# A row softmax on one core: whole-tile maxima, a broadcast multiplication in six tiles, and a new order for the last tiles

## Chip, cores and metric

One core of a Trainium2 chip. In the profiles DVE is VectorE, ACT is ScalarE and SP is SyncE; a q behind an engine (ACTq) marks its queue, from which its DMAs are issued. The metric is device time in microseconds (us) of one execution; 35 executions of the kernel before lay between 317.39 and 318.83 us, all but one within 0.3% of 317.7. "Span" is the profiled part of an execution, some 2 us shorter than the time.

## The reference

```python
x: (32, 512, 1024) float32;  temperature = 0.5

scaled  = x / temperature
shifted = scaled - max(scaled, axis=-1, keepdims=True)
exp_x   = exp(shifted)
return exp_x / sum(exp_x, axis=-1, keepdims=True)
```

16384 rows of 1024 numbers: 67.1 MB are read and 67.1 MB written.

## The kernel before

The rows are cut into 16 tiles of 128 partitions x 8 rows x 1024 (4 MB each), kept in six buffers. A tile is worked on in two groups of four rows. For each group DVE takes the maxima of the rows and makes a bias of them, ACT computes the exponentials row by row (in place, with the row's sum as a by-product), and DVE inverts the sums and multiplies each row. A tile goes out by one DMA, issued in ACT's queue; right after it in the program stands the load that reuses a buffer, in SP's queue.

```python
TILES = [[8]] * 16
BUFS = 6
GROUP = 4
...
    def maximum(g):
        ...
        nc.vector.tensor_reduce(out=top, in_=tiles[i][:, a : a + k, :], axis=..., op=extreme)
        nc.vector.tensor_scalar_mul(bias, in0=top, scalar1=-scale)

    def exponential(g):
        for b in range(k):
            nc.scalar.activation(tiles[i][:, a + b, :], tiles[i][:, a + b, :], Exp,
                                 bias=bias[:, b : b + 1], scale=scale, accum_out=sums[:, b : b + 1])

    def divide(g):
        nc.vector.reciprocal(recip, sums)
        for b in range(k):
            nc.vector.tensor_scalar_mul(tiles[i][:, a + b, :], in0=tiles[i][:, a + b, :],
                                        scalar1=recip[:, b : b + 1])

    def store(g):                      # after the last group of a tile
        nc.scalar.dma_start(out=dram(of, i)..., in_=tiles[i]...)
        load()                         # the next load, into a buffer that comes free
...
    nc.vector.addr_align(128, offset=0, max_nops=0)
    nc.scalar.addr_align(128, offset=0, max_nops=0)
    for _ in range(BUFS):
        load()
    for g in range(len(groups) + 1):
        if g < len(groups):
            maximum(g)
            exponential(g)
        if g > 0:
            divide(g - 1)
            store(g - 1)
```

So in program order the multiplication and the store of a group come behind the maximum and the exponentials of the next group.

## Time and profile before

| before | |
|---|---|
| time, median of 3 | 317.68 us (317.51 to 318.83) |
| span | 315.6 us |
| DVE busy | 235.5 us (75%) |
| ACT busy | 149.6 us (47%) |
| share of the span that the two DMA queues' packets took | 98.9% |

Most of the lines on which this reading rests are in the prediction below. To them belong the costliest groups and the DMA issues of the page. A group line has the source line, engine, operation, what is written and read, shape and count, then busy us and mean ns of one, then the idle time in front of it with what ended it. A DMA line has the size of one and the median time from issue to landing.

```profile
L70 DVE TENSOR_REDUCE top<-xt 128x4 f32<-128x4096 f32 x32 | 141.3, 4416 | 62.2 <-DMA xt<-in_x_dram 62.2
L93 DVE TENSOR_SCALAR xt<-xt,recip 128x1024 f32<-128x1024 f32 x128 | 87.7, 749 | 1.1
...
xt<-in_x_dram SPq DMA_DIRECT2D x16, 4096.0 KB, 50.2
out_dram<-xt ACTq DMA_DIRECT2D x16, 4096.0 KB, 38.4
```

The maxima are DVE's largest item, and in front of them DVE stands idle for 62.2 us in all, waiting for loads. A load takes 50 us to land although 4 MB at the 433 GB/s that before moved from 90 to 280 us are 9.7 us: it queues.

### The profile page before, as it was taken

What the parts mean: (1) busy time and instruction counts of PE and PEld (TensorE: products, weight loads), DVE (VectorE), ACT (ScalarE), POOL (GpSimd) and SP (SyncE); (2) the same over time, 40 slices, a digit from 0 to 9 for tenths busy, and PEclk for the clock granted to TensorE, in tenths of its full rate; (3) what the DMA queues carried; (4) which work ended last, traced back from release to release, by engine and by line L of the source; (5) the groups of instructions that cost most, each with busy time, mean ns of one, the idle gap of its engine ahead of it and who ended that gap; (6) DMA issues with size and microseconds to landing.
All of it is one profiled execution on the core that took longest, in us unless ns stands there. A gap on an engine that the chain in (4) does not pass through costs nothing.

```text
span 315.6 us, 622 instructions
## 1 busy us (share of the span) xinstructions
DVE 235.5 (75%) x224; ACT 149.6 (47%) x257; POOL 0.2 (0%) x4
## 2 busy tenths in 40 slices
DVE  0299999999789494994939949498594976949720
ACT  0176666666626255361553615546065560645500
POOL 0000000000000000000000000000000000000000
DMA  8999999999999999999999999999999999999996
GB/s 330 415 448 415 386 457 407 461 411 453 424 440 432 432 432 429 444 424 453 415 454 407 457 407 457 403 461 403 461 403 461 403 462 403 461 419 444 428 436 278
DMA packets 4613, 134.26 MB, mean 425 GB/s; under 512 B 512, under 2 KB 512, under 8 KB 512
## 3 DMA queue, kind: packets, MB, share of 16 engines
q1 hardware_dynamic: 2304, 67.11, 49.7%
q10 hardware_dynamic: 2304, 67.11, 49.2%
q14 instruction: 5, 0.04, 0.0%
HBM read 67.11 MB, written 67.11 MB: 425 GB/s over the span
## 4 chain that ended last, share of the span: by engine, by line
DVE 72%; another core or an unknown queue 15%; DMA 4%; ACT 3%; issue 1%; DVEq 0%
DVE top L70 43%; DVE xt L93 27%; DMA xt<-in_x_dram 4%; ACT xt L79 3%; DVE recip L91 1%; DVE bias L73 1%; DVEq L150 0%
## 5 line engine op out<-in xcount | busy, mean ns | idle before, releaser
L79 ACT ACTIVATE xt<-xt,bias 128x1024 f32<-128x1024 f32 x128 | 145.4, 1137 | 136.0 <-DVE recip L91 118.6
L70 DVE TENSOR_REDUCE top<-xt 128x4 f32<-128x4096 f32 x32 | 141.3, 4416 | 62.2 <-DMA xt<-in_x_dram 62.2
L93 DVE TENSOR_SCALAR xt<-xt,recip 128x1024 f32<-128x1024 f32 x128 | 87.7, 749 | 1.1
L79 ACT ACTIVATION_READ_ACCUMULATOR xt<-xt,bias 128x1 f32 x128 | 23.8, 186 | 0.0
L79 ACT ACT_TABLE_LOAD x1 | 1.3, 1283 | 13.5 <-DMA xt<-in_x_dram 13.5
L91 DVE RECIPROCAL recip<-sums 128x4 f32<-128x4 f32 x32 | 5.5, 171 | 2.1 <-ACT xt L79 2.1
L73 DVE TENSOR_SCALAR bias<-top 128x4 f32<-128x4 f32 x32 | 5.5, 170 | 1.1
L136 POOL MEMSET const-bfloat16-1.0<- 128x1 bf16 x1 | 0.1, 102 | 0.0
L136 POOL MEMSET const-uint8-127<- 128x1 uint8 x1 | 0.1, 102 | 0.0
L136 POOL MEMSET const-float32-0.0<- 128x1 f32 x1 | 0.1, 99 | 0.2 <-issue 0.2
L136 POOL MEMSET const-float32-1.0<- 128x1 f32 x1 | 0.1, 99 | 0.0
## 6 DMA issues: line engine op xcount, KB each, us to landing
xt<-in_x_dram SPq DMA_DIRECT2D x16, 4096.0 KB, 50.2
out_dram<-xt ACTq DMA_DIRECT2D x16, 4096.0 KB, 38.4
```

Source lines behind the costliest of these rows:

```text
L70: nc.vector.tensor_reduce(out=top, in_=tiles[i][:, a : a + k, :], axis=mybir.AxisListType.X, op=extreme)
L73: nc.vector.tensor_scalar_mul(bias, in0=top, scalar1=-scale)
L79: nc.scalar.activation(tiles[i][:, a + b, :], tiles[i][:, a + b, :], mybir.ActivationFunctionType.Exp, bias=bias[:, b : b + 1], scale=scal ...
L91: nc.vector.reciprocal(recip, sums)
L93: nc.vector.tensor_scalar_mul(tiles[i][:, a + b, :], in0=tiles[i][:, a + b, :], scalar1=recip[:, b : b + 1])
L136: nc = _bacc.Bacc("TRN2", target_bir_lowering=False, num_devices=1)
```

## The change

Its intent: fewer and longer instructions on DVE in the middle of the kernel, and at the end an order in which tile 13 and tile 14 are finished as soon as they can be. In tiles 2 to 13 the maximum is taken over all eight rows in one pass; in tiles 2, 4, .. 12 all eight rows are multiplied by one tensor_tensor with a broadcast factor; before tile 14 and before tile 15 the tile in front is divided and stored first; the two alignments (the addr_align lines) go.

```diff
-TILES = [[8]] * 16
+ROWS = 8
 BUFS = 6
-GROUP = 4
+PASSES = [[4, 4]] * 2 + [[8]] * 12 + [[4, 4]] * 2
+WHOLE = (2, 4, 6, 8, 10, 12)
+ALONE = 14
... (groups made from PASSES; a store still covers a whole tile)
     def divide(g):
         nc.vector.reciprocal(recip, sums)
+        if i in WHOLE:
+            xt = tiles[i][:, a : a + k, :]
+            nc.vector.tensor_mul(xt, xt, recip.unsqueeze(2).to_broadcast([P, k, d]))
+            return
         for b in range(k):
...
-        nc.vector.addr_align(128, offset=0, max_nops=0)
-        nc.scalar.addr_align(128, offset=0, max_nops=0)
         for _ in range(BUFS):
             load()
         for g in range(len(groups) + 1):
+            alone = g < len(groups) and groups[g][0] >= ALONE and groups[g][1] == 0
+            if g > 0 and alone:
+                divide(g - 1)
+                store(g - 1)
             if g < len(groups):
                 maximum(g)
                 exponential(g)
-            if g > 0:
+            if g > 0 and not alone:
                 divide(g - 1)
                 store(g - 1)
```

More of the change, by code (lines that the diff above doesn't have):

```diff
@@ L32 @@
     n, d = xf.shape
-    assert sum(sum(ks) for ks in TILES) * P == n
+    assert len(PASSES) * ROWS * P == n
     data = ctx.enter_context(tc.tile_pool(name="data", bufs=BUFS))
     stats = ctx.enter_context(tc.tile_pool(name="stats", bufs=4))
-    groups, first, r = [], [], 0
-    for i, ks in enumerate(TILES):
-        first.append(r)
-        r += sum(ks)
-        a = 0
-        for k in ks:
-            for b in range(0, k, GROUP):
-                m = min(GROUP, k - b)
-                groups.append((i, a + b, m, (a, k) if b + m == k else None))
-            a += k
+    groups = []
+    for i, ks in enumerate(PASSES):
+        assert sum(ks) == ROWS
+        for j, k in enumerate(ks):
+            groups.append((i, sum(ks[:j]), k))
     def dram(t, i):
-        k = sum(TILES[i])
-        block = t[P * first[i] : P * (first[i] + k), :]
-        return block.rearrange("(p k) d -> p k d", p=P, k=k)
+        block = t[P * ROWS * i : P * ROWS * (i + 1), :]
+        return block.rearrange("(p k) d -> p k d", p=P, k=ROWS)
     tiles, small = [], []
@@ L58, in load @@
         i = len(tiles)
-        if i < len(TILES):
-            xt = data.tile([P, sum(TILES[i]), d], f32, name="xt")
+        if i < len(PASSES):
+            xt = data.tile([P, ROWS, d], f32, name="xt")
             nc.sync.dma_start(out=xt, in_=dram(xf, i))
@@ L64, in maximum @@
     def maximum(g):
-        i, a, k, _ = groups[g]
+        i, a, k = groups[g]
         top, bias, sums, recip = (
@@ L75, in exponential @@
     def exponential(g):
-        i, a, k, _ = groups[g]
+        i, a, k = groups[g]
         bias, sums, _ = small[g]
@@ L88, in divide @@
     def divide(g):
-        i, a, k, _ = groups[g]
+        i, a, k = groups[g]
         _, sums, recip = small[g]
         nc.vector.reciprocal(recip, sums)
+        if i in WHOLE:
+            xt = tiles[i][:, a : a + k, :]
+            nc.vector.tensor_mul(xt, xt, recip.unsqueeze(2).to_broadcast([P, k, d]))
+            return
         for b in range(k):
@@ L97, in store @@
     def store(g):
-        i, _, _, part = groups[g]
-        if part:
-            a, k = part
-            nc.scalar.dma_start(out=dram(of, i)[:, a : a + k, :], in_=tiles[i][:, a : a + k, :])
-            if a + k == sum(TILES[i]):
-                load()
+        i, a, k = groups[g]
+        if a + k == ROWS:
+            nc.scalar.dma_start(out=dram(of, i), in_=tiles[i])
+            load()
     with tc.manual_schedule():
-        nc.vector.addr_align(128, offset=0, max_nops=0)
-        nc.scalar.addr_align(128, offset=0, max_nops=0)
         for _ in range(BUFS):
```

## The prediction

> **What bounds the kernel now.** I read the page first: the busy line, the slices, the queues.
>
> ```profile
> DVE 235.5 (75%) x224; ACT 149.6 (47%) x257; POOL 0.2 (0%) x4
> DVE  0299999999789494994939949498594976949720
> DMA  8999999999999999999999999999999999999996
> q1 hardware_dynamic: 2304, 67.11, 49.7%
> q10 hardware_dynamic: 2304, 67.11, 49.2%
> HBM read 67.11 MB, written 67.11 MB: 425 GB/s over the span
> ```
>
> No compute engine is near full, but the two DMA queues (loads on q1, stores on q10) took 49.7 + 49.2 = 98.9% of what 16 engines have in the span. Only 1.1% of 315.6 us, 3.5 us, is left, and both ends of the DMA row (8 and 6) use most of that up: nothing can move before the first issue, and the last bytes need a receipt.
>
> Then the chain of waits, which at first sight says the opposite.
>
> ```profile
> DVE 72%; another core or an unknown queue 15%; DMA 4%; ACT 3%; issue 1%; DVEq 0%
> 243.55 4.43 DVE top L70
> 251.03 4.34 DVE top L70
> 258.42 4.46 another core or an unknown queue
> 262.87 0.02 issue
> 262.90 4.43 DVE top L70
> ```
>
> 72% on DVE is where the trail was followed, not a bound: before each tile DVE stands still for 4.46 us. The waits name what it waits for:
>
> ```profile
> DVE top L70 <- DMA xt<-in_x_dram: 62.2, 12, 13.4
> SPq L61 <- DMA out_dram<-xt: 224.7, 10, 53.6
> ```
>
> One wait is the first load (13.4 us); the other eleven are (62.2 - 13.4)/11 = 4.4 us each, on loads. The load queue waits for stores to land, since a seventh load needs a buffer. From 107 us on a tile starts every 19.35 us (243.55 to 262.90): 8.39 MB in and out per tile / 19.35 us = 433 GB/s. DVE needs 19.35 - 4.48 = 14.9 us of it. So in the middle this is a copy at full DMA rate with slack on every engine.
>
> The end, from the timeline in order of time:
>
> ```profile
> 282.25 4.42 DVE L70 TENSOR_REDUCE top<-xt 128x4 f32<-128x4096 f32 x1 [4.49 <-DMA xt<-in_x_dram]
> 289.76 0.34 ACTq L101 DMA_DIRECT2D out_dram<-xt  x1
> 302.01 0.34 ACTq L101 DMA_DIRECT2D out_dram<-xt  x1
> ```
>
> The last load lands at 282.2; the last store is issued 19.76 us later and took 12.8 us (the shortest time to landing among the stores), so 314.8. Was DMA idle while the last tile was computed? From the 2 us windows from 302 us: 524, 459, 328, 524, 393, 180 GB/s, so 4.82 MB went after 302 us, 0.62 MB more than the last store: a backlog of 0.62/433 = 1.4 us was still there. The DMA was fed to the end, only just.
>
> [...]
>
> **The change, part by part.**
>
> 1. Maximum over 8 rows at once in tiles 2 to 13. Before: 2 x 4416 = 8.83 us and two bias computations. [...] DVE gains about 0.3 us a tile and an equal trifle for one reciprocal less; both in slack.
>
> 2. Multiplication in tiles 2, 4, .. 12. Before: 8 x 0.685 (four take 2.74 us in the chain) = 5.48 us. After: one tensor_tensor with a broadcast factor[...]: 3.2 us more in each of six tiles. DVE per tile becomes 8.69 + 0.3 + 8.69 = 17.7 us in those and 8.69 + 0.3 + 5.48 = 14.5 us in the others, mean 16.1. Against 19.35 us there is still slack, 1.7 us even in the worst tile, and cost on the path is zero. DVE busy in all falls by some 12 x 0.4 us and rises by 6 x 3.2 us: about +14 to +18 us, counting that busy time of short multiplies overlaps.
>
> 3. Later stores in the middle. ACT issues store i-1 behind all its exponentials of tile i: 8 x 1.135 us (pace in the timeline) = 9.1 us. So the store leaves at 8.69 + 0.3 + 9.1 = 18.2 us after tile i's landing, before 7.5 (243.55 to 251.06): 10.7 us later. (The tensor_tensor, 8.7 us beside 9.1 us of exponentials, ends just in time.) A buffer's round is 6 x 19.35 = 116 us. Before it was 50.2 (load) + 19.35 + 7.5 + 38.4 (store) = 115.5. After, 116 - 37.6 = 78.6 us are left for load and store, which at half rate need 2 x 19.4 plus a few us. Both queues keep a queue.
>
> 4. The start, where the store queue may run dry. Until 40.4 us nothing changes. DVE then: tile 2's maximum to 49.1, tile 1's second multiply to 52.1, exponentials of tile 2 to 58.4, store 1 issued there instead of 47.9. Store 0 lands at about 57.2 (the load queue's first wait), so the store queue is empty for about 3.4 us. The load queue isn't: loads 4 and 5 are still coming (tile 5 lands at 87.9). The DMA stays full; loads get about 3.4 us ahead, stores 3.4 us behind. Next stores: 2 at 70.1, 3 at 87.8, 4 at 102.4, while store 1 lands at about 80, 2 at 99, 3 at 119: no further gap.
>
> 5. The end. Loads are 3.4 us ahead: tile 13 lands at 240.2, 14 at 259.5, 15 at 278.9. Tile 13 is finished before tile 14 starts: 240.2 + 18.2 + 0.2 + 5.5 = store 13 at about 264. That holds DVE 4.8 us beyond the landing of tile 14; its maxima end at 273.3, exponentials at 278, last multiply at 281.1: store 14 there, before 289.8. Tile 15 starts at 281.1, 1.1 us before the old 282.2, and its store leaves at 281.1 + 19.76 = 300.9, before 302.0. What does DMA have then? Store 11 lands at about 80 + 10 x 19.4 = 274; store 12 is a quarter done at 278.9, and without loads a store takes 9.7 us: 12 ends at 286, 13 at 296, 14 at 305.6, 15 at 315.3. The same sum for before (store 1 at 76.6) gives 315.2, where 314.8 was measured. So the last store comes in time, with a larger backlog than before, and the end doesn't move.
>
> 6. Alignment and fewer instructions: the chain has one fetch gap on DVE near the end (DVEq 0.2%, 0.66 us), in the tail where the backlog is 1.4 us. At most a few tenths of a us.
>
> Sum: 0 + 0 + 0 + 0 + (0 to -0.5) = about 317.4 us from 317.68.
>
> **The rivals.** (a) Starvation: later stores free buffers later, so loads come late, and the end moves with the last load. For it: the store leaves 10.7 us later, and in before a load was issued 31 us ahead of its predecessor's landing (50.2 - 19.35). Against it: about 20 us of that lead remain. If a load did come 1 us late in each of 12 tiles, 330 us. (b) DVE becomes the bound: if the broadcast form ran at half the assumed speed, 17.4 us, a pair of tiles would need 26.4 + 14.5 = 40.9 us against 38.7: six pairs x 2.2 = some 8 to 13 us more, 326 to 331. Nothing in before has a tensor_tensor[...]. (c) The tail: if the backlog of 1.4 us in fact hid an idle stretch at 302 to 304 us, the earlier last store gives up to 1 us: 316.6. (d) The mix: the load-only start ran at about 425 GB/s, the store-only end at about 440, the mix at 433. The change lengthens both one-sided stretches by the same bytes, so they cancel to some 0.1 us.
>
> **Range and chances.** DMA busy at 98.9% leaves at most 3.5 us (1.1%), so 2% faster (311.3) would need a rate of 440 GB/s over everything. 2% slower (324) needs 6 us of idle DMA, thus (a) or (b), 2% together. Between them the run-to-run spread (317.51 to 318.83) is larger than any term of mine. Time 317.4, range 316.4 to 318.8; faster 0.01, same 0.97, slower 0.02.
>
> **What would show it.** Right: DMA row 9 throughout, both queues together 98 to 99%, DVE busy near 250 us. The tensor_tensor near 8.7 us x6 and the reduce near 8.7 x12; DVE still waiting on loads before tiles 6 to 13, by 1 to 5 us; stores leaving about 18 us after the landing of the next tile; the last tile's maximum at 279 to 282 and the last store at about 301. Wrong: a DMA slice of 8 or less in the middle, DVE with no waits there (then rival b), load times to landing near 20 us (rival a), or a last store well after 303 with an empty slice before it.

The 8.69 us that the sums use for eight rows' maxima and for the tensor_tensor stand without what they were derived from. From before's trace alone, twice 4416 ns would give 8.83 us for the maxima, and nothing there shows a tensor_tensor. The changed kernel then took 8685 ns in the mean of 12 maxima and 8692 ns in that of 6 multiplications. The rates in (d) are before's from 2 to 32 us (425), from 284 to 312 us (440) and from 90 to 280 us (433).

## The result, and the profile after

| | before | after |
|---|---|---|
| time, median of 6 | 317.75 us (317.51 to 318.83) | 317.30 us (317.22 to 317.74) |
| span of the profiled run | 315.6 | 316.0 |
| DVE busy, us | 235.5 | 251.0 |
| DVE waits for loads, first load left out, us | 48.8 | 31.3 |

The ratio of after to before is 0.9983, 95% interval 0.9969 to 0.9998. Here and below a ratio is the mean time of one kernel's fast runs over that of the other's fast runs of the same rounds, so not quite the ratio of the medians quoted. The difference is far inside the 2% within which two kernels count as the same.

From the page of the changed kernel: busy times, the slices of DVE and DMA, and the two queues.

```profile
DVE 251.0 (79%) x146; ACT 148.1 (47%) x257; POOL 0.2 (0%) x4
...
DVE  0399999999689794997939979299793999979710
...
DMA  8999999999999999999999999999999999999996
...
q1 hardware_dynamic: 2304, 67.11, 49.8%
q10 hardware_dynamic: 2304, 67.11, 49.2%
```

The DMA row is the same as before, digit for digit, and the queues still take 99% of 16 engines' span. DVE does 15.5 us more work (251.0 - 235.5) and its waits for loads are 17.5 us shorter (48.8 - 31.3): the longer multiplication fell into time in which DVE had been waiting. Its groups, and the wait in question:

```profile
L68 DVE TENSOR_REDUCE top<-xt 128x8 f32<-128x8192 f32 (+1 forms) x20 | 139.5, 6976 | 44.6 <-DMA xt<-in_x_dram 44.6
L95 DVE TENSOR_SCALAR xt<-xt,recip 128x1024 f32<-128x1024 f32 x80 | 54.3, 749 | 0.5
L92 DVE TENSOR_TENSOR xt<-xt,recip 128x8192 f32<-128x8192 f32 x6 | 52.2, 8692 | 0.2
```

One tensor_tensor over 8192 elements takes 8692 ns. The mean of the maxima mixes two shapes; the timeline has 8.69 us for eight rows, as in its first line below. It shows tile 13, then the last tile and the last two stores (start, duration, engine, line, operation):

```profile
243.86 8.69 DVE L68 TENSOR_REDUCE top<-xt 128x8 f32<-128x8192 f32 x1 [4.92 <-DMA xt<-in_x_dram]
...
284.24 4.41 DVE L68 TENSOR_REDUCE top<-xt 128x4 f32<-128x4096 f32 x1
284.36 0.34 ACTq L102 DMA_DIRECT2D out_dram<-xt  x1
...
301.13 0.34 ACTq L102 DMA_DIRECT2D out_dram<-xt  x1
```

Tile 13 starts when it did before (243.55) and still waits for its load. The last tile is now kept back by DVE, not by its load (no wait is noted), and the last store leaves at 301.1 instead of 302.0. One detail differs from what the prediction had assumed, and it is seen where store 1 leaves:

```profile
49.21 1.15 ACT L77 ACTIVATE xt<-xt,bias 128x1024 f32<-128x1024 f32 x1 [7.07 <-issue]
...
51.49 1.13 ACT L77 ACTIVATE xt<-xt,bias 128x1024 f32<-128x1024 f32 x1
51.90 8.68 DVE L68 TENSOR_REDUCE top<-xt 128x8 f32<-128x8192 f32 x1
52.02 0.34 ACTq L102 DMA_DIRECT2D out_dram<-xt  x1
...
57.15 1.13 ACT L77 ACTIVATE xt<-xt,bias 128x1024 f32<-128x1024 f32 x1
```

The store stands behind eight exponentials in ACT's program, yet it is issued during the third of them, at the moment when the multiplication ends (52.0), and the eighth starts at 57.15.

### The profile page after: what moved, and what is told of

Its sections match the earlier page's. It is cut to its first block, busy times and chain, and to the rows that moved or that the text cites. A ratio compares the mean times of both kernels' runs of the same rounds, so it can differ in the third digit from the quotient of the medians.

```text
span 316.0 us, 530 instructions
## 1 busy us (share of the span) xinstructions
DVE 251.0 (79%) x146; ACT 148.1 (47%) x257; POOL 0.2 (0%) x4
## 3 DMA queue, kind: packets, MB, share of 16 engines
q10 hardware_dynamic: 2304, 67.11, 49.2%
## 5 line engine op out<-in xcount | busy, mean ns | idle before, releaser
L68 DVE TENSOR_REDUCE top<-xt 128x8 f32<-128x8192 f32 (+1 forms) x20 | 139.5, 6976 | 44.6 <-DMA xt<-in_x_dram 44.6
L95 DVE TENSOR_SCALAR xt<-xt,recip 128x1024 f32<-128x1024 f32 x80 | 54.3, 749 | 0.5
L92 DVE TENSOR_TENSOR xt<-xt,recip 128x8192 f32<-128x8192 f32 x6 | 52.2, 8692 | 0.2
L89 DVE RECIPROCAL recip<-sums 128x8 f32<-128x8 f32 (+1 forms) x20 | 3.7, 187 | 4.1 <-ACT xt L77 4.1
L71 DVE TENSOR_SCALAR bias<-top 128x8 f32<-128x8 f32 (+1 forms) x20 | 3.4, 170 | 0.7
## 6 DMA issues: line engine op xcount, KB each, us to landing
xt<-in_x_dram SPq DMA_DIRECT2D x16, 4096.0 KB, 49.7
```

What stands on the lines that cost most here:

```text
L92: nc.vector.tensor_mul(xt, xt, recip.unsqueeze(2).to_broadcast([P, k, d]))
```

## The experiments

The theory is that the time is a copy of 134 MB at the DMA's rate and computing is hidden. Against it stand: that the engines' hand-overs set part of it, that the new order at the end or another single part made the small gain, and the prediction's first two rivals, starvation by later stores and DVE as the bound. Twelve runs were made (e12 is the changed kernel again); those that give a wrong output are named. Only four of them (e5, e6, e8, e10) move the time by more than 0.4%: e5 takes up DVE's slack, e6 and e8 have fewer buffers, and in e10 the last store leaves late.

### e1_copy_only: no computing at all

Its output is wrong, which doesn't matter for the time.

```diff
-                maximum(g)
-                exponential(g)
...
-                divide(g - 1)
                 store(g - 1)
```

> All computing taken out: the 16 loads and 16 stores of the changed kernel alone (the output is the input, wrong on purpose). Theory DMA (the time is 134.2 MB at about 433 GB/s plus a start and a receipt, computing is hidden): 316 to 317.5 us, at most 0.5% below before. Rival PACING (DVE or the hand-over between engines sets part of the time, and DMA queues merely look full because records cover waiting): clearly below 312 us. The order of loads and stores differs (stores can start at 13 us, not at 33), which may move it by some tenths either way.

Measured: 316.64 us (316.60 to 316.72), ratio 0.9967 (0.9955 to 0.9978). The DMA part of its page:

```profile
DMA  8999999999999999999999999999999999999997
...
q1 hardware_dynamic: 2304, 67.11, 49.9%
q10 hardware_dynamic: 2304, 67.11, 49.4%
```

Taking away all computing gains 1.1 us against before and 0.7 us against the changed kernel. So with these tiles, buffers and queues computing costs the changed kernel about 0.2% (the order of loads and stores differs too, so this is not exact to a tenth). The rival that computing paces the kernel falls. The start and the receipt of the expectation are in the packet records: the first packet starts at about 1.7 us, and the last store is reported as landed at 314.1, 0.3 us after its last packet ended (313.7). In before the same two are 1.74 us and 0.35 us (314.82 against 314.47).

### e2_late_store1: the prediction's own mistake made real

```diff
     def divide(g):
...
+        if i == 1 and a + k == ROWS:
+            for b in range(k):
+                if b == k - 1:
+                    invert(g + 1)     # reciprocal of tile 2: waits for all its exponentials
+                nc.vector.tensor_scalar_mul(tiles[i][:, a + b, :], ...)
+            return
```

> The changed kernel, but the last row of tile 1 is multiplied only behind all exponentials of tile 2, so that store 1 leaves at about 59 us instead of 52, after store 0 has landed (57.2): the dry store queue that the prediction wrongly put into the changed kernel. Theory DMA (a dry store queue is used by the loads): DVE is some 7 us late at tile 3 and has caught up by tile 8; tile 13's maximum starts 3 to 5 us earlier than the changed kernel's 243.9, at 239 to 241; the time is unchanged, 317.0 to 317.8 us. Rival LOST (DMA time in which only one queue has work is lost in part): 3 to 4 us more, 320 to 321 us, and tile 13 not earlier.

Measured: 317.67 us (317.21 to 318.60), ratio 1.0002 (0.9988 to 1.0016). Store 1 left at 59.1 instead of 52.0. Tile 13's maximum and the last store in the timeline:

```profile
237.94 8.69 DVE L68 TENSOR_REDUCE top<-xt 128x8 f32<-128x8192 f32 x1 [5.18 <-DMA xt<-in_x_dram]
...
295.20 0.34 ACTq L119 DMA_DIRECT2D out_dram<-xt  x1
```

Tile 13 starts 5.9 us earlier than in the changed kernel (237.94 against 243.86), a little more than the 3 to 5 expected: while the store queue was empty, the loads used its share (from 34 to 60 us the DMA moved 417 GB/s at a share of 0.99, in the changed kernel 417 at 1.00). The packet records of the kept trace show the gap: no packet of a store is in flight from 56.2 to 62.5 us, 6.3 us (in the changed kernel 0.7 us at the same place). Store 1 was issued at 59.1, and its first packet started 3.4 us later. The last store also leaves 5.9 us earlier (295.2 against 301.1), and the time doesn't move. It only waits longer behind other stores: the shortest time to landing of a store is 20.8 us here, 14.0 in the changed kernel. Here loads and stores traded places without loss, and an earlier last store was worth nothing while a backlog of stores was there.

### e3_alone_only, e4_passes_no_alone, e11_passes_only, e9_no_align: single parts

```diff
# e3: before, plus the new order at the end
+            alone = g < len(groups) and groups[g][0] >= 14 and groups[g][1] == 0
+            if g > 0 and alone:
+                divide(g - 1)
+                store(g - 1)
# e4: the changed kernel without it
-ALONE = 14
+ALONE = 99
# e11: before, plus whole-tile maxima only (e4 with the alignments kept, and)
-WHOLE = (2, 4, 6, 8, 10, 12)
+WHOLE = ()
# e9: before, without the alignments
-        nc.vector.addr_align(128, offset=0, max_nops=0)
-        nc.scalar.addr_align(128, offset=0, max_nops=0)
```

> The kernel before plus only the new order at the end (tile 13 and tile 14 finished before the next tile starts). Theory TAIL (the 0.4 us that the changed kernel gained come from the last store leaving earlier): last store at about 299 to 301 us, time 317.2 to 317.4, ratio near 0.998. Rival NOISE or another part: ratio 1.000 within 0.001, 317.6 to 317.9 us. Theory DMA in its strict form also says the second.

> The changed kernel without the new order at the end: whole-tile passes, tensor_tensor in six tiles, no alignment. Theory TAIL: ratio 1.000, the last store back near 302 to 304 us (tile 14's second multiply again between the maxima of tile 15, 2.7 us). Rival: if the gain comes from the middle or the missing alignment it stays, ratio near 0.998.

> The kernel before plus only the maximum over eight rows in tiles 2 to 13 (alignment kept, rows multiplied one by one, old order at the end). The changed kernel, the one without the new end and the one with five buffers lay at 317.2 to 317.3, those with passes of four rows at 317.6 to 318.0. Theory PASSES (the whole-tile passes bring 0.1%): 317.2 to 317.4, ratio 0.998 to 0.9995 with an interval below 1. Rival NOISE: interval holds 1.

> The kernel before with the two alignments taken out and nothing else. Theory NOISE (the alignments do nothing that counts): ratio 1.000 within 0.0015, 317.5 to 318.0 us, and the 0.66 us fetch gap of DVE near the end stays. Rival FETCH (the changed kernel's 0.4 us come from there): ratio near 0.998.

| kernel | us, median (range) | ratio to before (95% interval) | last store issued |
|---|---|---|---|
| e3, new order at the end only | 317.88 (317.46 to 318.22) | 1.0005 (0.9993 to 1.0017) | 299.6 |
| e11, whole-tile maxima only | 317.93 (317.49 to 318.02) | 1.0004 (0.9992 to 1.0017) | 302.5 |
| e9, no alignment only | 317.97 (317.90 to 318.50) | 1.0014 (1.0001 to 1.0027) | 301.9 |
| e4, all but the new order | 317.26 (317.02 to 318.26) | 0.9991 (0.9979 to 1.0003) | 301.6 |

None of three parts alone makes the kernel faster; without the alignment it was, if anything, a trifle slower. The theory that the earlier last store brings the gain falls: in e3 the last store left 2.4 us ahead of the 302.0 of before, without a gain. e4 is inconclusive, since its interval holds both 1 and the changed kernel's ratio.

### e12_after_again: is the small gain real?

The changed kernel unchanged, five rounds more.

> The changed kernel itself once more. If its 0.17% are real: ratio 0.998 to 0.9995, interval below 1, last store at about 301 us. If they were noise: the interval holds 1.

Measured: 317.14 us (317.02 to 317.51), ratio 0.9986 (0.9972 to 0.9999), last store at 300.4. Twice the interval lies just below 1, so a gain of some 0.15% (0.5 us) seems to be there. Which part or combination makes it stays open: the tensor_tensor was not run alone. The medians of the changed kernel, e12, e4 and e7 below, which all have the tensor_tensor and no alignment, are 317.1 to 317.3, those of before, e3, e9 and e11 317.6 to 318.0; but e2, which has both features too, lay at 317.7, so this hint settles nothing.

### e5_double_multiply: the slow broadcast form of rival (b)

Its output is wrong, which doesn't matter for the time.

```diff
             nc.vector.tensor_mul(xt, xt, recip.unsqueeze(2).to_broadcast([P, k, d]))
+            nc.vector.tensor_mul(xt, xt, recip.unsqueeze(2).to_broadcast([P, k, d]))
```

> The changed kernel with the whole-tile multiplication of tiles 2, 4 .. 12 done twice (wrong on purpose in those tiles): the slow broadcast form of the prediction's rival (b), 17.4 us instead of 8.7. Theory SLACK (DVE has about 1.6 us to spare in such a tile and 5 in the others, nothing more): a pair of tiles needs 26.4 + 14.4 = 40.8 us of DVE against 38.7 of DMA, and DVE chains through from tile 2 at 40.2 us: tile 14 starts some 20 us later than 267.5, the last store at about 321, time 334 to 338 us, DVE without waits for loads after tile 5. The prediction's own figure for this rival was 326 to 331. Rival HIDDEN (DVE matters nowhere): 317 us.

Measured: 334.33 us (334.14 to 334.49), ratio 1.0526 (1.0512 to 1.0540). Its wait for loads, and two stretches near the end (us, then busy time of DVE, ACT and POOL, clock, DMA share, GB/s):

```profile
DVE top L68 <- DMA xt<-in_x_dram: 13.2, 1, 13.2
```

```profile
310.00:315.00 5.00, 4.75 (x6) 5.00 (x9) 0.00 (x0) 1.00 0.73 315
315.00:320.00 5.00, 3.33 (x6) 2.77 (x6) 0.00 (x0) 1.00 0.00 0
```

Only the first load is waited for: DVE's slack is used up. The six extra multiplications are 6 x 8.69 = 52.1 us of work; 31.3 us of it fitted into the waits that the changed kernel still had, and the rest, 20.8 us, agrees with the delay of the last store (320.80 against 301.13, 19.7 us). By then the DMA has nothing left to do: it stands still from 315 to 320 us. So DVE is hidden as far as the slack of 31.3 us goes, to about 1 us. The time rose by less, 17.0 us (334.33 - 317.30), because the last store no longer waits behind others: it lands after 11.1 us instead of 14.0.

### e6_bufs4, e7_bufs5, e8_before_bufs4: how much lead the buffers hold

```diff
-BUFS = 6
+BUFS = 4        # e6: the changed kernel; e8: the kernel before.  e7: the changed kernel with 5
```

> The changed kernel with four buffers instead of six. Theory RING: a buffer's round is 4 x 19.35 = 77.4 us, 34 to 37 of it between landing and issue of the store, so 40 to 43 us remain for a load and a store that share the DMA and need some 42 with their latencies: queues run dry for 1 to 3 us a tile, time 325 to 350 us. Rival (late stores cost nothing whatever the buffers): 317 to 319 us.

> The changed kernel with five buffers. Theory RING: 5 x 19.35 = 96.8 us, less 34 to 37, leaves about 60 us for a load and a store that need some 42: both queues keep work, time unchanged, 317.0 to 318.0 us, the loads' median time to landing about 19 us shorter than 49.7. Rival (the lead was spent by the later stores, six buffers are just enough): over 320 us.

> The kernel before with four buffers. Theory HOLD (the changed kernel lost 3% with four buffers because it keeps a tile 7 to 10 us longer between landing and store): before keeps it 26.9 us of the 77.4, which leaves 50.5 for a load and a store that took 22 each in the changed kernel with four buffers; only the start, where the loads run dry until store 0 lands, costs 1 to 3 us: 317.5 to 321 us. Rival (four buffers are too few whatever the order of work): as the changed kernel, 325 to 330 us.

Measured: e7 317.24 us (317.15 to 317.35), ratio 0.9988 (0.9972 to 1.0003): the sixth buffer isn't needed. Loads took 31.4 us to landing in the median, 18.3 less than with six, as a round shorter by one tile demands. e6 328.47 us (325.21 to 329.49), ratio 1.0324 (1.0280 to 1.0368): within the range that RING expected. e8 323.56 us (323.48 to 326.26), ratio 1.0206 (1.0173 to 1.0238): between the two expectations, so neither was right. The middle of the changed kernel with six buffers, then two stretches of e6, the middle first:

```profile
90.00:280.00 190.00, 161.32 (x82) 90.29 (x157) 0.00 (x0) 1.00 1.00 432
```

```profile
90.00:280.00 190.00, 154.10 (x74) 85.92 (x151) 0.00 (x0) 1.00 1.00 421
...
305.00:310.00 5.00, 3.33 (x7) 2.68 (x6) 0.00 (x0) 1.00 0.99 426
```

and the same stretches of e8:

```profile
90.00:280.00 190.00, 143.17 (x137) 91.32 (x158) 0.00 (x0) 1.00 1.00 433
...
305.00:310.00 5.00, 2.92 (x5) 1.77 (x4) 0.00 (x0) 1.00 0.49 210
```

The two lose in different places. e6 loses before the end: 421 GB/s where the changed kernel with six buffers had 432 in the same stretch (and 409 against 433 from 40 to 90 us), with its load and store times to landing down to 22 us each, and nothing at the end. (The DMA share stays at 1.00 in the middle, so the records show packets that took longer rather than engines that stood still. The queues did run dry, but one at a time: from 40 to 280 us each of the two has no packet in flight for about 58 us, where the changed kernel has 5 and 2. From 90 to 280 us 144 of 1256 load packets took over 1.4 us, where the changed kernel has 13 of 1257; why they took longer is open. The profiled run, 325.21 us, was also the fastest of the four, so more may be lost in others.) e8 keeps its 433 in the middle, as the theory of the shorter hold had it, and loses at the end, which that theory had left out: with four buffers its stores take 23.9 us to landing instead of 38.4, so few stores are left over when the last load lands (290.0), and while the last tile is computed the DMA falls to 210 GB/s in two of the four stretches of 5 us from 290 to 310. So the backlog of stores that covers the last tile's computing depends on the buffers.

### e10_store_first: one line moved in ACT's program

```diff
                 maximum(g)
+                if g > 0 and not alone:
+                    divide(g - 1)
+                    store(g - 1)
                 exponential(g)
-            if g > 0 and not alone:
+            elif g > 0:
                 divide(g - 1)
                 store(g - 1)
```

> The changed kernel with one line moved: in ACT's program the store of tile i-1 stands ahead of the exponentials of tile i, not behind them; DVE's program is the same. Theory ORDER (ACT's queue passes its instructions in program order and a store in it waits for the multiply, while exponentials that were already handed to the engine don't hold a later store): exponentials of a whole tile start only at the end of the multiply, 6 to 9 us later than now; nothing happens in the middle, but tile 13's exponentials end at about 271 instead of 262, its multiply at 276 instead of 267.5, the last store leaves at about 310 and the time is 322 to 325 us. Rival FREE (the issue of a store isn't ordered with ACT's computing at all): exponentials still start right behind the bias and the time is 317.3 us.

Measured: 323.49 us (323.32 to 323.59), ratio 1.0182 (1.0169 to 1.0196). The first line is store 1, the second the first exponential of tile 2:

```profile
52.35 0.34 ACTq L102 DMA_DIRECT2D out_dram<-xt  x1
52.79 1.15 ACT L77 ACTIVATE xt<-xt,bias 128x1024 f32<-128x1024 f32 x1 [10.59 <-DVE xt L95]
```

The exponentials now start behind the store (52.8 instead of 49.2) and wait for the multiplication. The middle doesn't notice (433 GB/s from 90 to 280 us). At the end the last store leaves at 309.81, as expected (310), and from 305 to 310 us the DMA moves nothing:

```profile
309.81 0.34 ACTq L102 DMA_DIRECT2D out_dram<-xt  x1
```

```profile
305.00:310.00 5.00, 3.10 (x6) 1.79 (x4) 0.00 (x0) 1.00 0.00 0
```

So in e10 the store that waited for the multiplication (52.35) held back the exponentials behind it (52.79), while in the changed kernel the store at 52.02 was issued with five of the eight exponentials in front of it not yet started.

## Why the prediction was right, and where its steps were not

The time (317.4 forecast, 317.3 measured) and its main reason hold: e1 shows the floor of the copy 0.7 us below, e2 that the two queues trade work without loss, and e5 that DVE had slack, of the size that the trace of the changed kernel shows.

- Step 1, right: 8.69 us for eight rows' maxima in the timeline, the figure in the prediction's sums. Before's trace by itself gave 8.83.
- Step 2, right: 8692 ns measured, where the sums have 8.69 us, for which before's trace showed nothing; DVE's busy time rose by 15.5 us, between the 14 and 18 forecast, and it still waits for tiles 6 to 13, by 1.6 and about 5 us in turn, which is the slack that follows from the step's sums (19.35 - 17.7 = 1.7 and 19.35 - 14.5 = 4.9).
- Step 3, right in the verdict, wrong in the mechanism. "ACT issues store i-1 behind all its exponentials of tile i" isn't what happens: stores leave when the multiplication ends, about 18 us after the landing for a tensor_tensor tile (store 2 at 69.70, tile 3 at 51.90), where the two moments coincide, but 14.5 us behind it for the others (tile 8 and store 7 below). The buffers' round therefore had more room than was counted for every other tile.

```profile
146.28 8.69 DVE L68 TENSOR_REDUCE top<-xt 128x8 f32<-128x8192 f32 x1 [1.64 <-DMA xt<-in_x_dram]
...
160.74 0.34 ACTq L102 DMA_DIRECT2D out_dram<-xt  x1
```

The profile of before had it in view. Its store at 251.06 stands behind the four exponentials of a group, of which the last started after it:

```profile
251.06 0.34 ACTq L101 DMA_DIRECT2D out_dram<-xt  x1
...
251.67 1.13 ACT L79 ACTIVATE xt<-xt,bias 128x1024 f32<-128x1024 f32 x1
```

- Step 4, wrong: with store 1 at 52.0 and not 58.4 the store queue had its next store 5.7 us before store 0 had landed (the load that waits for store 0 was issued at 57.7), so the loads didn't get 3.4 us ahead: tile 13 started at 243.9, not at 240.2. e2 shows that the inference from such a gap was sound all the same, but the gap's size was not: the step's own 58.4 and 57.2 are 1.2 us apart, not 3.4, and in e2, with store 1 at 59.1, it was 6.3 us and the loads' lead 5.9.
- Step 5, right by two errors that cancel. The last tile began at 284.2 instead of 281.1, because the loads were not ahead, and took 301.13 - 284.24 = 16.9 us instead of 19.76, because the second multiplication of tile 14 (2.74 us) no longer stands between its two maxima, which the step overlooked. Hence 301.1 against 300.9: that this number came true was luck, and the start at 284.2 lies outside the 279 to 282 that the prediction had named as a sign of being right. Its sum for the DMA held, and the time rests on that rather than on the issue of the last store: it has the last store landed at 315.3, and 301.1 + 14.0 is 315.1. Its backlog of 1.4 us in before is rough, because the 2 us windows from which it was read swing between 328 and 524 GB/s.
- Step 6, right as far as it goes: the gap of 0.66 us on DVE is still there without the alignment (at 299.99 in before, 299.11 in the changed kernel, 299.90 in e9), and e9 shows no gain. The trace puts it down to DVE's queue (DVEq); that it is a fetch was not shown.
- Rival (a) needs far less buffer than there is: five are enough, four are not. Rival (b) was real but undersized: 326 to 331 forecast for a form of 17.4 us, 334 measured. It gave six pairs of tiles a slack of 38.7 - 17.7 - 14.5 = 6.5 us each, 39 us in all; the trace of the changed kernel has 31.3, since DVE waits for no load between the first tile and tile 5. Rival (c) falls with e2 and e3, whose last stores left earlier without a gain. Rival (d)'s claim that one-sided stretches cost nothing agrees with e2.

## What to carry to other kernels

Before an engine's instruction is made longer or shorter, add up its waits for data. Here 15.5 us more work, below a sum of 48.8 us, was hidden; in e5 52.1 us more, 20.8 us beyond the 31.3 us of waits that were left, gave 19.7 us of delay of the last store and 17.0 us of time. In a copy-bound kernel run the copy alone first: it says how much all further work on the engines can bring (here 0.7 us). And look at what the DMA has left to do when the last load lands; in these runs buffers, order and late stores mattered there first.
